# Queue orders of the middle norm in a hybrid diffusion layer: output chunks of the second half one by one, the urgent accumulator of the head units first

## The chip, the cores and the metric

One core of one Trainium2 chip. The metric is the device time of one execution in microseconds (us), the median over runs. The engines are PE (TensorE, matmuls), PEld (its weight loads), DVE (VectorE), ACT (ScalarE), POOL (GpSimd) and SP (SyncE, which issues the DMAs). Each works off its own queue in order and waits on semaphores for the others.

## The reference, cut to what matters

One layer over 128 context tokens and 512 latent tokens, width 1024. The stretch of this document lies between the two sub-layers:

```python
mod = silu(cond) @ w_ada + b_ada
sh1, sc1, g1, sh2, sc2, g2 = split(mod, 6)
...
mix = concatenate([y_ssd, u], -1) @ w_out
x = x + g1 * rms_norm(mix, norm_mix_post)
h = rms_norm(x, norm_ffn_pre) * (1 + sc2) + sh2
up = h @ w_ffn_up
up = dwconv(up)                       # 3x3 on the latent grid, 3 on the context
f = (silu(f_gate) * f_val) @ w_ffn_down
x = x + g2 * rms_norm(f, norm_ffn_post)
```

Everything is float32; the large products are made of three matmuls of split operands (high x high, high x low, low x high), so that they keep the precision.

## The kernel before, in words

Data lie transposed: 128 channels on the partitions, 640 tokens along them. A column chunk m (0 to 7) is 128 of the 1024 output channels. The tokens come in two halves, half 0 with 384 and half 1 with 256.

**The weights.** Each unit of 1024 columns is loaded by SP into `wr` (two buffers), copied by ACT into `wh` (L311), and the remainder is written to `wl` by POOL or DVE (L313). A full matmul (L415 in `mm3`, L1259 in `up_mm`) takes a 128 x 128 block of wh or wl. The units of this stretch, by the numbers that the tiles carry: wh57 and wh60 belong to chunks 3, 4 and 5, 6 of half 1 (part y), wh58, wh59, wh61, wh62 and wh64 are chunks 3 to 7 of half 1 (part u), wh63 is part y of chunk 7; wh65 to wh69 are the five head units of the up-projection; wh70 onwards are the later up units.

**The output projection and the middle norm.** For each half the chunks 3 to 7 are summed in PSUM (`y_part`, 9 matmuls, and `u_part`, 24), evicted by DVE (L1072, `out_done`), squared by ACT (L1077) and the squares added by POOL (L1079). Then, for the half:

- `msum`: column sum of the squares on PE (L473), root on ACT (L487), reciprocal on DVE (L488);
- `spread`: the row is spread over the partitions on PE (L481);
- `x2`: for each m a scaling on DVE (L1156), an add of the residual (L1158, on POOL for m = 2 and 5), a square on ACT (L1159);
- `xsum`, root, reciprocal and `spread` again;
- `h2`: for each k a scaling on DVE (L1176), the high part on ACT (L1178), the low part on DVE (L1183).

The steps for half 0 lie between the output chunks of half 1, and those for half 1 between the matmuls of the head. The head is the first five units of the up-projection; for half 0 they use the banks ps2 (unit 0), ps0, ps1, and for half 1 unit 0 uses ps2, unit 1 ps0, unit 2 ps1 and units 3 and 4 the narrow banks pq0 and pq1. Unit 0, 1 and 2 are convolved by DVE straight from PSUM (ACT L1227 starts, then ten taps, L1237 to L1240); units 3 and 4 are copied (L1262) and convolved aside by ACT and POOL (L1305, L1306). The next full unit (wh70) takes ps2 again.

**Narrow matmuls.** The adaLN products (`ada_half`, L460) and the column sums (`colsum`, L473) have only 32 output rows and are placed on one of four strips of 32 columns of the array, four strips in turn:

```python
for j in range(4):
    te.matmul(pt[32 * j:32 * j + 32, 0:P], cts[:, kc, :], w[:, j * P:(j + 1) * P],
              start=kc == 0, stop=kc == KD - 1, tile_position=(0, 32 * j))
```

**What sets the order.** Each engine's instructions are numbered in the order in which the program writes them, and `ORDER` says for each engine in which order they are issued; `issue_in_order` chains each to the one before it. In PE's order, 2927-2958 are the adaLN product 3, 2993-3024 product 4, 3059-3090 product 5 and 3539-3570 product 6; 3176-3183 and 3380-3387 are `msum` of half 0 and half 1, 3254-3269 with 3285-3300 and 3455-3470 with 3477-3492 their `xsum`; 3199-3202, 3328-3331, 3406-3409 and 3505-3508 the spreads. The chunks of half 1 are 3158-3198 (m=3), 3203-3235 (m=4), 3236-3284 (m=5), 3301-3337 (m=6) and 3338-3370 (m=7), as far as those numbers are not in the lists before. 3371-3538 are the head for half 0, 3572-3595 unit 0 for half 1, 3596-3619 unit 3, 3620-3643 unit 4, 3644-3667 unit 1, 3668-3691 unit 2; 3692-3739 is the unit of wh70.

Of the kernel before, what the change touches and what calls it, by code (L numbers as in the profile page):

```python
# [37 lines left out]
for _name, _w in (("b_ada", 48), ("g_mix_pre", 8), ("g_mix_post", 8), ("g_ffn_pre", 8),  # L38
# [37 lines left out]
2712 2683-2686 2718-2727 2687-2689 2728 2713 2729-2740 2714 2690-2692 2830-2831 2771-2780 2832-2835  # L76
2781-2790 2836-2841 2843 2741-2742 2715-2716 2792-2794 2743-2747 2791 2748-2755 2844-2847 2756-2758
2795-2799 2848-2849 2800-2809 2850-2860 2894-2896 2960-2963 2897-2915 2964-2966 2916-2924 2967-2973
2925-2926 2974-2987 2861-2892 2842 3092-3094 3026 2988-2990 3027-3035 2991-2992 3036-3045 3095 3046-3057
3096-3099 2893 3058 3125 3100-3102 2927-2942 2993-3014 2943-2950 3015-3024 2951-2958 3103-3107 2959  # L80
3108-3122 3126-3133 3123-3124 3134-3146 3203-3204 3147-3150 3025 3151-3158 3059-3089 3176-3183 3090
3159-3165 3205-3207 3166-3175 3184-3188 3208-3210 3189-3198 3211-3218 3199-3202 3091 3219-3236 3301-3310
3237-3245 3311 3246-3251 3312 3252-3253 3270-3276 3313-3317 3338 3318-3319 3277-3284 3320-3327 3332-3337
3339-3348 3254-3269 3285-3300 3328-3331 3349-3373 3388-3390 3397-3398 3380-3387 3374-3375 3399 3410-3412
3406-3409 3377 3376 3391-3393 3400-3402 3413-3415 3419 3422-3423 3378 3420 3379 3394-3396 3421 3403-3405
3424 3431 3416-3418 3425 3428 3426 3429 3432-3433 3430 3437-3439 3446-3448 3427 3434-3436 3471-3476 3443
3440-3442 3449-3451 3493-3504 3509-3510 3444-3445 3452 3511-3513 3539-3556 3455-3470 3477-3492 3514-3524
# [15 lines left out]
448-450 405-407 443 408-410 421-422 444 411 424 423 451 445-446 412-413 426 414-415 425 427 454 429-430 455  # L103
452-453 434 439 436 438 435 456 433 457 437 440 460 431 459 458 461-462 441 466-467 469-470 472 478 473
475-476 468 479-480 482-485 481 471 474 488 477 486 489 487 495 498 496 502 501 497 491 490 505 508 494
499-500 515 509 503-504 518 492 512 493 519 506-507 510-511 520-522 537 523 513-514 516 525 527-528 530 526
529 532-533 538 531 535 524 540 534 557 536 539 517 541-543 545 544 558 546 548 550 547 559 552 560-561
563-564 566 549 551 567 565 553 568 554-556 569 571-575 570 562 576-585 589 586-588 593 590 594 591-592 595
597 596 598 601-602 599-600 605 603-604 606-612 615-616 613-614 617-749 1053 750-1046 1049-1051 1047-1048
1052 1054-1063 1065 1064 1066-1075""",  # L110
    "Activation": """
0-3 7 6 4 8 5 9-11 15 18 12 19 17 21-22 13 20 24 23 25 35 26-27 32-33 14 30 28-29 16 48-49 47 31 56-58 61 64
50-51 62 34 67 65-66 63 52-53 37-38 79 116 80 54 36 39 55 71 68 40-43 120 44-45 72 46 117 121-122 81 69-70
# [14 lines left out]
498-499 494 502 496 491 497 493 505-506 509 500-501 503 507 510-511 504 512-514 516 515 508 525-526 528-529
527 521 517-518 532 519-520 531 523 522 524 530 542 541 533-536 544 543 550 537 545 538-540 547 546 559 551
548 553-554 560 556 555 549 552 557-558 561-565 568-569 566-567 570 578 571-577 581 579 583 580 603-605  # L130
609-611 582 584 588 585 615-616 632 617 586 621-622 633 590 589 634 587 643-644 638 592 623 591 645 639-640
596 593 649 624 650 598 594 597 601 599 651 595 652 606 600 602 613 607 612 608 618 614 625 619-620 627 626
630 628-629 635 631 641 636-637 646 642 653 647-648 655 654 658 656-657 660 659 663 661-662 665 664 668
666-667 670 669 673 671 675 672 674 678 676 680 677 679 683 681 685 682 684 688 686 690 687 689 693 691 695
692 694 698 696 700 697 699 703 701 727 705 702 704 708 706 709 707 714 710-713 715 719 716 725-726 717 720
731 718 723 721-722 732 724 728-729 733-734 730 735 741 736-740 745 742-744 746-747 751 748-750 752-753 757
754-756 758-759 763 760-762 764-765 769 766-768 770-771 775 772-774 776-784""",
    "Pool": """
0-13 16-19 14-15 24-25 20 26-27 33 21-23 65 69 28-30 35 70 36 34 75 51 93 31 37-42 32 49 43 50 44-48 71 97
52-59 98 64 66 72 67 77 60 76 61 73 62-63 74 80 103-104 99 78-79 81-84 92 68 105 100 85-88 94 89 123 108 90  # L140
# [4 lines left out]
219-223 239-240 224-227 241-243 232-233 244-245 234-236 246-248 251-252 249 255 250 256 253-254 257-261
264-265 267-268 262-263 266 269-270 272 271 273-274 279 275 280 276-278 281-282 294-295 300 298 285 299 303
302 304 283 315 307 286 284 316 308 287 319 309 321 320 290 324 310 323 291 325 328-329 288 293 330 289 331
296 292 301 305 297 311-312 306 314 317 313 322 326 318 332-333 327 335-336 334 338-339 337 341-342 340
344-345 343 347-348 346 350-351 349 353-354 352 356-357 355 359-360 358 362-363 361 365-366 364 367-369 372
370 373-374 371 375-377 379 378 380-381 383 382 384-385 387 386 388-389 391 390 392-393 395 394 396-397 399  # L150
398 400-411""",
    "SP": """
0-8 14 24 10 13 16 11 9 12 15 23 19 17 31 27 25 18 20 26 28-29 41 47 30 36 34-35 38 40 21 43 39 37 44-45 42
46 48-49 22 50 32-33 53 52 54-57 72 81 51 59-61 82 58 64 62 83 63 87 96 68 67 97 65-66 69 98 75-76 74 70 73
# [1442 lines left out]
```

## Time and profile before

| | |
|---|---|
| median of 3 runs | 983.82 us (982.83 to 984.3) |
| span of the profiled execution | 979.4 us |
| PE busy | 944.5 us, 96% of the span |
| DVE, ACT, POOL busy | 686.9, 471.3, 577.9 us |
| stretch that the new orders cover | about 451 to 554 us of the span |

The profiled execution's own time outside the span is not listed, so its span stands beside the median of the runs. In the profile a row of the timeline gives the start (us from the span's start), the busy time, the engine, the line, the operation, output and inputs by the program's names (without buffer numbers), the shape, and how many alike were merged; in brackets the idle time before it and what ended it. A narrow float32 matmul leaves two records.

### The profile page before, as it was taken

The numbers are of one execution on the slowest core, as the hardware profiler recorded it, in microseconds if no ns is written. First come the engines' busy times: TensorE is split into PE (matmuls) and PEld (weight loads), VectorE is DVE, ScalarE is ACT, GpSimd is POOL, SyncE is SP. The second block draws the span as 40 slices with busy tenths as digits, with TensorE's granted clock in tenths as the row PEclk, the third lists the DMA queues.
The fourth block names the chain that finished last, engine by engine and source line by source line (L and its number), as shares of the span: only waits on it lengthen the run. The fifth ranks groups of instructions, "written<-read, shape, count | busy, mean of one in ns | idle before, by whom it ended". The sixth has DMA issues, their size and how long they took to land.

```text
span 979.4 us, 18795 instructions
## 1 busy us (share of the span) xinstructions
PE 944.5 (96%) x7623; PEld 920.9 (94%) x7623; DVE 686.9 (70%) x1076; ACT 471.3 (48%) x799; POOL 577.9 (59%) x416
## 2 busy tenths in 40 slices
PE   4999999999999999999999999999999999999995
PEld 3799999999999998998889999999999999999995
DVE  1769898999989997523585998998988898400004
ACT  4355666877668477622464852323232336322211
POOL 1334699889999882534662994444454436543434
PEclk9999999999999999999999999999999999999998
DMA  9622424433424422578662322222222231322213
GB/s 347 250 72 86 117 82 127 146 95 123 139 80 142 128 91 93 196 244 303 200 218 88 129 86 69 84 78 73 86 66 86 66 87 54 94 69 76 82 38 108
DMA packets 50294, 117.52 MB, mean 120 GB/s; under 512 B 6016, under 2 KB 13952, under 8 KB 50208
## 3 DMA queue, kind: packets, MB, share of 16 engines
q1 hardware_dynamic: 50208, 116.33, 37.2%
q8 instruction: 60, 0.98, 0.4%
q14 instruction: 26, 0.21, 0.1%
HBM read 112.55 MB, written 3.75 MB: 119 GB/s over the span
## 4 chain that ended last, share of the span: by engine, by line
PE 87%; DMA 3%; ACT 3%; DVE 2%; SPq 1%; POOL 1%; issue 1%; POOLq 0%; ACTq 0%; DVEq 0%
PE ps L415 72%; PE ps L1259 3%; PE pq L415 2%; PE pq L818 2%; PE pq L807 1%; PE pq L460 1%; SPq L452 1%; DMA wr<-in_wout 1%; PE pq L744 1%; PE pq L441 1%; POOL wl L313 1%; PE pq L473 1%; DMA S<-acD 1%; ACT wh L311 1%; DMA T<-in_wada 1%
## 5 line engine op out<-in xcount | busy, mean ns | idle before, releaser
L313 POOL TENSOR_TENSOR wl<-wr,wh 128x1024 fp32r<-128x1024 f32 (+3 forms) x127 | 290.4, 2290 | 316.3 <-ACT wh L311 299.2
L415 PE MATMUL ps<-H,wh 128*128 128x384 f32 (+1 forms) x1636 | 315.7, 309 | 0.1
L311 ACT ACTIVATE wh<-wr 128x1024 fp32r<-128x1024 f32 (+3 forms) x131 | 131.3, 1003 | 316.2 <-PE ps L415 183.2
L415 PE MATMUL ps<-T,wh 128*128 128x384 f32 (+1 forms) x1472 | 272.5, 306 | 1.8 <-ACT S L1227 1.8
L1237 DVE SCALAR_TENSOR_TENSOR S<-ps,prms,S 128x441 f32<-128x441 f32 (+2 forms) x336 | 233.5, 695 | 29.4 <-ACT S L1227 18.9
L415 PEld LDWEIGHTS ps<-H,wh 128*128 128x128 f32 x1636 | 249.0, 188 | 2.7 <-issue 1.7
L415 PEld LDWEIGHTS ps<-T,wh 128*128 128x128 f32 x1472 | 218.9, 188 | 2.2 <-ACT S L1227 2.1
L872 DVE SCALAR_TENSOR_TENSOR ps<-u,prms,ps 128x655 f32<-128x655 f32 x205 | 185.1, 903 | 10.8 <-ACT ps L869 4.8
L415 PE MATMUL ps<-H,wl 128*128 128x384 f32 (+1 forms) x818 | 191.8, 309 | 0.0
L415 PE MATMUL ps<-T,wl 128*128 128x384 f32 (+1 forms) x736 | 166.2, 305 | 0.0
L415 PEld LDWEIGHTS ps<-H,wl 128*128 128x128 f32 x818 | 129.0, 188 | 1.0 <-issue 1.0
L415 PEld LDWEIGHTS ps<-T,wl 128*128 128x128 f32 x736 | 113.0, 188 | 0.0
L488 DVE RECIPROCAL rsm<-rsm 128x160 f32<-128x160 f32 (+2 forms) x9 | 7.4, 817 | 147.1 <-ACT rsm L487 147.1
L415 PE MATMUL ps<-S,wh 128*128 128x384 f32 (+1 forms) x420 | 88.0, 310 | 1.6 <-ACT wh L311 1.6
L415 PEld LDWEIGHTS ps<-S,wh 128*128 128x128 f32 x420 | 66.5, 188 | 2.8 <-ACT wh L311 1.8
L415 PE MATMUL ps<-S,wl 128*128 128x384 f32 (+1 forms) x210 | 54.9, 309 | 0.3 <-POOL wl L313 0.3
L789 ACT ACTIVATE S<-S,AC 128x128 f32<-128x128 f32 x140 | 45.5, 392 | 2.4 <-DMA S<-acD 2.4
L885 POOL TENSOR_TENSOR T<-T,T 128x640 f32<-128x640 f32 x20 | 32.0, 1602 | 12.5 <-ACT T L881 12.5
L1227 ACT ACTIVATE S<-ps,prms 128x640 f32<-128x640 f32 x42 | 36.5, 869 | 0.0
L415 PEld LDWEIGHTS ps<-S,wl 128*128 128x128 f32 x210 | 35.2, 188 | 0.9 <-POOL wl L313 0.5
L881 ACT ACTIVATE T<-u,prms 128x512 f32<-128x512 f32 (+1 forms) x54 | 27.9, 554 | 6.8 <-POOL T L885 6.8
L1339 POOL TENSOR_TENSOR H<-S,S 128x640 f32<-128x640 f32 x16 | 25.3, 1581 | 0.0
(346 smaller groups left out, 1180.3 us busy)
## 6 DMA issues: line engine op xcount, KB each, us to landing
wr<-in_wup SPq DMA_DIRECT2D x44, 512.0 KB, 3.5
wr<-in_win SPq DMA_DIRECT2D x36, 512.0 KB, 3.9
T<-in_wada SPq DMA_DIRECT2D x49, 256.0 KB, 5.4
S<-acD SPq DMA_DIRECT2D x28, 320.0 KB, 4.7
wr<-in_wdown SPq DMA_DIRECT2D x16, 512.0 KB, 3.4
wr<-in_wout SPq DMA_DIRECT2D x13, 512.0 KB, 4.5
H<-in_wada SPq DMA_DIRECT2D x23, 256.0 KB, 4.6
S<-in_wada SPq DMA_DIRECT2D x16, 256.0 KB, 5.4
```

Source lines behind the costliest of these rows:

```text
L311: ac.activation(hi[:, :n], raw[:, :n], AF.Copy)
L313: lo_eng.tensor_tensor(lo[:, :n], raw[:, :n], hi[:, :n].bitcast(F32), SUB)
L415: last_mm[0] = te.matmul(out, w, x[:, c0:c1], start=first and i == 0, stop=last and i == 2)
L789: ac.activation(rc, rc, AF.Relu, scale=-1.0, bias=AC2[:, c, row:row + 1])
L818: te.matmul(py[64 * h:64 * h + 64, i * P:(i + 1) * P], xt[:, c * P + 64 * h:c * P + 64 * h + 64], rs[h, d][:, c * P:(c + 1) * P], start=d ...
L872: ve.scalar_tensor_tensor(acc, u[:, j:j + UO], w(j), acc, MUL, ADD)
L881: ac.activation(t[:, b:c], u[:, a:a + c - b], AF.Copy, scale=w(j))
L885: gp.tensor_tensor(far, far, t, ADD)
L1227: ac.activation(out, v, AF.Identity, bias=prm_col("ffn_b", i), scale=w(1, 1))
L1237: ve.scalar_tensor_tensor(ob, vl[:, r0 + a - 1:r1 + a - 1, q0 + b - 1:q1 + b - 1], w(a, b), ob, MUL, ADD)
L1259: te.matmul(pt[:, o:o + c1 - c0], w[k] if i in (1, 2) else w[:, k * P:(k + 1) * P], x[:, c0:c1], start=k == 0 and j == 0, stop=k == KD - 1 ...
L1339: gp.tensor_tensor(f_raw[q], a, b, MUL)
```

## The change

Only the lists of `ORDER` change; every instruction, its operands and its engine stay. The five lists are laid out anew between about 451 and 554 us. In PE's list chunk 5 of half 1 is issued as a whole ahead of chunk 6; unit 0 of the head for half 1 is issued further ahead of units 1 to 4; narrow and full matmuls are mixed in another way. In ACT's list the eviction of unit 0 (579) stands ahead of the split of wh70 (581), and the squares of the norm (517-524) and the splits (529, 532) are ordered anew. In DVE's list the adds of x2 (524 to 536), the eviction of chunk 7 (558) and the parts of h2 are ordered anew. In SP's list the loads of adaLN product 5 (228-235) and 6 (262-269) and of the residual (237-244, 258-260) move against the weight loads (247-275). The diff, cut:

```diff
     "PE": """
 ...
-2925-2926 2974-2987 2861-2892 2842 3092-3094 3026 2988-2990 3027-3035 2991-2992 3036-3045 3095 3046-3057
-3096-3099 2893 3058 3125 3100-3102 2927-2942 2993-3014 2943-2950 3015-3024 2951-2958 3103-3107 2959
-3108-3122 3126-3133 3123-3124 3134-3146 3203-3204 3147-3150 3025 3151-3158 3059-3089 3176-3183 3090
-3159-3165 3205-3207 3166-3175 3184-3188 3208-3210 3189-3198 3211-3218 3199-3202 3091 3219-3236 3301-3310
-3237-3245 3311 3246-3251 3312 3252-3253 3270-3276 3313-3317 3338 3318-3319 3277-3284 3320-3327 3332-3337
-3339-3348 3254-3269 3285-3300 3328-3331 3349-3373 3388-3390 3397-3398 3380-3387 3374-3375 3399 3410-3412
 ...
-3440-3442 3449-3451 3493-3504 3509-3510 3444-3445 3452 3511-3513 3539-3556 3455-3470 3477-3492 3514-3524
-3505-3508 3557-3570 3525-3538 3453-3454 3572-3575 3644-3647 3668-3669 3576-3578 3648-3650 3670-3674
 ...
-3624-3625 3591-3593 3596-3598 3594-3595 3599-3619 3626-3643 3660-3667 3683-4059 4061-4081 4060 4082-5548
 ...
+3096-3097 3057 3098-3099 3058 3100 2927 3101 2928-2930 2893 2931-2932 3102 2933-2934 3125 2935-2941
+2993-2998 2942 2999-3008 2943 3009-3015 2944 3016-3018 2945-2950 3019-3024 2951-2952 3103 2953-2957 3104
+2958 3105-3107 2959 3108-3115 3126 3116-3122 3127 3123 3128 3124 3129-3146 3203 3147-3148 3204 3149-3150
+3025 3151-3156 3059 3157 3060-3070 3158 3071-3077 3176-3177 3078-3089 3178 3090 3179-3181 3159 3182 3160
+3205 3183 3206 3161-3165 3207 3166-3168 3208 3169-3175 3184-3188 3209-3210 3189 3211 3190-3192 3199
+3193-3198 3212 3200 3213-3218 3201-3202 3091 3219 3236 3220-3235 3237-3243 3301 3244-3253 3270-3283
+3302-3304 3284 3305-3317 3338 3318-3327 3332 3339 3333 3340-3342 3254-3255 3334-3335 3343 3336-3337
+3344-3347 3256-3266 3348 3267-3269 3285-3300 3328-3331 3349-3373 3388-3390 3397-3398 3380-3381 3374
+3382-3387 3375 3399 3410-3412 3406 3377 3407-3408 3376 3391-3392 3409 3393 3400-3402 3413-3415 3419 3378
 ...
+3437-3439 3446-3448 3427 3434-3436 3471-3473 3443 3539 3474 3540 3475-3476 3440 3541-3545 3493-3498
+3546-3551 3441-3442 3552 3449-3450 3499-3503 3455-3457 3504 3509-3510 3444-3445 3511 3553-3554 3512
+3555-3556 3452 3458-3460 3513 3451 3461-3470 3557 3477-3490 3515 3491-3492 3516 3514 3517-3523 3505-3508
+3558-3565 3524 3566-3567 3525 3568-3569 3526-3527 3570 3528-3535 3453 3536-3537 3454 3572 3538 3573
 ...
+3653-3655 3620 3656 3675-3676 3621 3677 3622-3623 3657-3658 3678 3585 3679 3586-3593 3596-3597 3594-3595
+3680 3624 3598-3605 3681 3606 3625 3607-3608 3659 3609-3613 3626 3614-3618 3660 3619 3627-3634 3682
+3635-3637 3661-3662 3638-3641 3663-3666 3683-3684 3642 3685-3688 3667 3689-3690 3692 3691 3693-3712 3643
+3713-3737 3740-3742 3738 3743-3751 3739 3752-4059 4061-4081 4060 4082-5548 5597-5615 5549-5596 5616-5658
 ...
     "DVE": """
 ...
-529 532-533 538 531 535 524 540 534 557 536 539 517 541-543 545 544 558 546 548 550 547 559 552 560-561
+529 538 532-535 540 531 536 539 516 557 517 541-543 545 558 544 546 548 550 547 559 549 552 551 560-561 563
     "Activation": """
 ...
+498-499 494 502 496 491 497 493 505 500 506 501 503 507 509 504 510-514 516 515 508 525-526 528 517 520 529
+519 523 527 518 531-532 521-522 524 530 542 533 535 541 534 544 536 543 550 545 537 539 538 540 546-547 551
+559 553 555-556 548 557 554 552 558 560-561 549 562-563 567-568 566 565 564 571-572 570 569 573 575 578 577
+574 576 579 581 580 603 605 604 584 611 609 583 616 610 615 586 617 621 585 588 582 632-633 590 589 634 587
 ...
     "SP": """
 ...
-212 246 209 223-225 218 220-222 247-248 240 239 237 231 229-230 228 234 249 233 235 242 232 250-251 243 238
+212 246 209 223-225 218 220-222 229 247 231 241 248 230 228 238 235 233-234 249 232 242 240 239 250-252 244
 ...
```

More of the change, by code (lines that the diff above doesn't have):

```diff
@@ L83 @@
-3237-3245 3311 3246-3251 3312 3252-3253 3270-3276 3313-3317 3338 3318-3319 3277-3284 3320-3327 3332-3337
-3339-3348 3254-3269 3285-3300 3328-3331 3349-3373 3388-3390 3397-3398 3380-3387 3374-3375 3399 3410-3412
-3406-3409 3377 3376 3391-3393 3400-3402 3413-3415 3419 3422-3423 3378 3420 3379 3394-3396 3421 3403-3405
-3424 3431 3416-3418 3425 3428 3426 3429 3432-3433 3430 3437-3439 3446-3448 3427 3434-3436 3471-3476 3443
-3440-3442 3449-3451 3493-3504 3509-3510 3444-3445 3452 3511-3513 3539-3556 3455-3470 3477-3492 3514-3524
@@ L88 @@
-3505-3508 3557-3570 3525-3538 3453-3454 3572-3575 3644-3647 3668-3669 3576-3578 3648-3650 3670-3674
-3579-3581 3571 3651-3653 3582-3584 3654-3656 3675-3680 3585-3587 3657-3659 3681-3682 3620-3623 3588-3590
-3624-3625 3591-3593 3596-3598 3594-3595 3599-3619 3626-3643 3660-3667 3683-4059 4061-4081 4060 4082-5548
-5597-5615 5549-5596 5616-5658 5693-5695 5659-5664 5696-5716 5665-5692 5717-6599 6665-6668 6600-6664
-6669-6676""",
+2925-2926 2974-2987 2861-2892 2842 3092-3094 3026 2988-2990 3027-3035 2991-2992 3036-3045 3095 3046-3056
@@ new lines @@
+3193-3198 3212 3200 3213-3218 3201-3202 3091 3219 3236 3220-3235 3237-3243 3301 3244-3253 3270-3283
+3302-3304 3284 3305-3317 3338 3318-3327 3332 3339 3333 3340-3342 3254-3255 3334-3335 3343 3336-3337
+3344-3347 3256-3266 3348 3267-3269 3285-3300 3328-3331 3349-3373 3388-3390 3397-3398 3380-3381 3374
+3382-3387 3375 3399 3410-3412 3406 3377 3407-3408 3376 3391-3392 3409 3393 3400-3402 3413-3415 3419 3378
+3420 3422-3423 3379 3394-3396 3421 3403-3405 3416 3424 3431 3417-3418 3425 3428 3426 3429 3432-3433 3430
@@ new lines @@
+3437-3439 3446-3448 3427 3434-3436 3471-3473 3443 3539 3474 3540 3475-3476 3440 3541-3545 3493-3498
+3546-3551 3441-3442 3552 3449-3450 3499-3503 3455-3457 3504 3509-3510 3444-3445 3511 3553-3554 3512
+3555-3556 3452 3458-3460 3513 3451 3461-3470 3557 3477-3490 3515 3491-3492 3516 3514 3517-3523 3505-3508
+3558-3565 3524 3566-3567 3525 3568-3569 3526-3527 3570 3528-3535 3453 3536-3537 3454 3572 3538 3573
+3668-3669 3574-3575 3644-3647 3576-3578 3648-3650 3670-3674 3579-3580 3651 3581 3652 3582 3571 3583-3584
@@ new lines @@
+3653-3655 3620 3656 3675-3676 3621 3677 3622-3623 3657-3658 3678 3585 3679 3586-3593 3596-3597 3594-3595
+3680 3624 3598-3605 3681 3606 3625 3607-3608 3659 3609-3613 3626 3614-3618 3660 3619 3627-3634 3682
+3635-3637 3661-3662 3638-3641 3663-3666 3683-3684 3642 3685-3688 3667 3689-3690 3692 3691 3693-3712 3643
+3713-3737 3740-3742 3738 3743-3751 3739 3752-4059 4061-4081 4060 4082-5548 5597-5615 5549-5596 5616-5658
+5693-5695 5659-5664 5696-5716 5665-5692 5717-6599 6665-6668 6600-6664 6669-6676""",
@@ L105 @@
 475-476 468 479-480 482-485 481 471 474 488 477 486 489 487 495 498 496 502 501 497 491 490 505 508 494
-499-500 515 509 503-504 518 492 512 493 519 506-507 510-511 520-522 537 523 513-514 516 525 527-528 530 526
-529 532-533 538 531 535 524 540 534 557 536 539 517 541-543 545 544 558 546 548 550 547 559 552 560-561
-563-564 566 549 551 567 565 553 568 554-556 569 571-575 570 562 576-585 589 586-588 593 590 594 591-592 595
-597 596 598 601-602 599-600 605 603-604 606-612 615-616 613-614 617-749 1053 750-1046 1049-1051 1047-1048
-1052 1054-1063 1065 1064 1066-1075""",
+499-500 515 509 492-493 503-504 512 518 506-507 519 510-511 520-522 537 523 525 513 527-528 530 524 526 514
+529 538 532-535 540 531 536 539 516 557 517 541-543 545 558 544 546 548 550 547 559 549 552 551 560-561 563
+562 564 566-567 553-556 568-569 571-572 574-577 565 579-580 573 578 581 570 582-588 590-591 598 589 592 601
+594 593 595 597 596 599-600 603-604 602 607 610 609 608 612 615 605-606 613 611 616 614 617-749 1053
+750-1046 1049-1051 1047-1048 1052 1054-1063 1065 1064 1066-1075""",
     "Activation": """
@@ L127 @@
 452-453 455 454 484-485 457 469-470 487 459 486 456 466 460 468 458 461-462 467 463-464 488-489 492 490 495
[L128 to L137, printed above, removed]
+498-499 494 502 496 491 497 493 505 500 506 501 503 507 509 504 510-514 516 515 508 525-526 528 517 520 529
+519 523 527 518 531-532 521-522 524 530 542 533 535 541 534 544 536 543 550 545 537 539 538 540 546-547 551
+559 553 555-556 548 557 554 552 558 560-561 549 562-563 567-568 566 565 564 571-572 570 569 573 575 578 577
+574 576 579 581 580 603 605 604 584 611 609 583 616 610 615 586 617 621 585 588 582 632-633 590 589 634 587
+643-644 622 638 592 623 591 645 639-640 596 593 649 624 650 598 594 597 601 599 651 595 652 606 600 602 613
+607 612 608 618 614 625 619-620 627 626 630 628-629 635 631 641 636-637 646 642 653 647-648 655 654 658
+656-657 660 659 663 661-662 665 664 668 666-667 670 669 673 671 675 672 674 678 676 680 677 679 683 681 685
+682 684 688 686 690 687 689 693 691 695 692 694 698 696 700 697 699 703 701 727 705 702 704 708 706 709 707
+714 710-713 715 719 716 725-726 717 720 731 718 723 721-722 732 724 728-729 733-734 730 735 741 736-740 745
+742-744 746-747 751 748-750 752-753 757 754-756 758-759 763 760-762 764-765 769 766-768 770-771 775 772-774
+776-784""",
     "Pool": """
@@ L144 @@
 182 228 193-195 204 196-199 206-207 231 200-201 230 229 208 213 202-203 216 212 237-238 215 217-218 214
[L145 to L151, printed above, removed]
+219-223 239-240 224-227 241-243 232-233 244-245 234-236 246-248 251-252 249 255-256 250 253-254 257 259 258
+260-261 264-265 267 262 268 263 270 266 269 272 271 273-275 279 276 280 277-278 281 294-295 300 298 303 282
+299 302 285 315 304 307 283 286 284 316 308 287 319 309 321 320 290 324 310 323 291 325 328-329 288 293 330
+289 331 296 292 301 305 297 311-312 306 314 317 313 322 326 318 332-333 327 335-336 334 338-339 337 341-342
+340 344-345 343 347-348 346 350-351 349 353-354 352 356-357 355 359-360 358 362-363 361 365-366 364 367-369
+372 370 373-374 371 375-377 379 378 380-381 383 382 384-385 387 386 388-389 391 390 392-393 395 394 396-397
+399 398 400-411""",
     "SP": """
@@ L159 @@
 198-199 191 182 197 189 183 200 217 211 204 261 210 215 207 226-227 216 206 202 208 213 205 214 236 245 219
-212 246 209 223-225 218 220-222 247-248 240 239 237 231 229-230 228 234 249 233 235 242 232 250-251 243 238
-241 252-254 244 255-256 267 263 257 270 258 260 259 271-272 264-265 269 262 266 268 273-274 276 278 280 282
-275 277 279 284 281 283 285-343 345 344 346 348 347 349 351 350 353 352 354 356 355 357 359 358""",
+212 246 209 223-225 218 220-222 229 247 231 241 248 230 228 238 235 233-234 249 232 242 240 239 250-252 244
+243 237 253-257 270 266 268 262 258 271 267 264 272 269 259 263 265 260 273-275 284-285 283 278 280-281
+286-287 277 279 282 288 276 289-343 345 344 346 348 347 349 351 350 353 352 354 356 355 357 359 358""",
 }
```

## The prediction

> **What bounds the kernel now.** I read the page first, then all of PE's waits in the stretch that the change touches, then windows and the timeline of one engine at a time.
>
> ```profile
> span 979.4 us, 18795 instructions
> ...
> PE pq L460 <- DMA T<-in_wada: 2.0, 3, 1.0
> PE ps L415 <- ACT S L1227: 1.8, 1, 1.8
> PE ps L415 <- ACT wh L311: 1.6, 1, 1.6
> PE pq L481 <- DVE gs L1127: 1.2, 1, 1.2
> PE ps L415 <- POOL wl L313: 0.3, 1, 0.3
> ...
> 500.00:541.00 41.00, 40.73 (x397) 39.24 (x396) 29.15 (x75) 21.88 (x49) 17.88 (x11) 1.00 0.47 153
> ```
>
> The span ends 979.4 us after its start; the median of the runs is 983.82, so 4.4 us lie around the span, and I add every change of the span to 983.82. The rows with arrows are those of PE between 450 and 545 us (total, times, longest): 6.9 us, all that better queue orders could win there. The last row is a window: its length, then the busy time of PE, PEld, DVE, ACT and POOL, the granted clock, the DMA share and GB/s. PE is busy for 40.73 of its 41 us, at the full clock: what is added to PE there has no cover. Behind 554 us the orders are the old ones and PE goes on without a gap, so a shift at 542 us goes through to the end.
>
> **Part 1, chunks one by one.** In half 1 the old PE order starts m=6 with ten matmuls, the tenth of which needs the weights wh62, and only then goes on with m=5, whose weights had been there.
>
> ```profile
> 483.45 0.50 PE L415 MATMUL ps<-S,wh 128*128 128x256 f32 x2 [1.59 <-ACT wh L311]
> 486.01 0.39 PE L415 MATMUL ps<-S,wl 128*128 128x256 f32 x1 [0.28 <-POOL wl L313]
> 482.34 1.06 ACT L311 ACTIVATE wh<-wr 128x1024 fp32r<-128x1024 f32 x1 [1.96 <-DMA wr<-in_wout]
> 479.45 0.40 PE L415 MATMUL ps<-H,wh 128*128 128x256 f32 x2
> 479.69 0.28 PE L415 MATMUL ps<-H,wl 128*128 128x256 f32 x1
> ```
>
> The new order puts 32 more matmuls of m=5 ahead of that tenth, at 0.12 us each (479.45 to 479.69 is two): 3.8 us of cover for a wait of 1.59, and the 0.28 behind it goes too. PE gains up to 1.9 us. SP issues the load of wr62 as soon as wl60 is made, as before; a load that I find 0.5 to 1 us earlier or later (SP now holds behind two releases of adaLN tiles) stays inside this cover.
>
> **Part 2, the urgent accumulator first.** Unit 0 sits in ps2, the bank that the next full unit needs.
>
> ```profile
> 533.78 0.27 PE L1259 MATMUL ps<-T,wl 128*128 128x256 f32 x1
> 534.03 1.06 ACT L311 ACTIVATE wh<-wr 128x1024 fp32r<-128x1024 f32 x1 [3.60 <-issue]
> 535.00 0.87 ACT L1227 ACTIVATE S<-ps,prms 128x640 f32<-128x640 f32 x1
> 535.90 5.81 DVE L1237 SCALAR_TENSOR_TENSOR S<-ps,prms,S 128x441 f32<-128x441 f32 x8 [4.23 <-ACT S L1227]
> 542.00 0.35 DVE L1240 SCALAR_TENSOR_TENSOR S<-ps,prms,S 128x127 f32<-128x127 f32 x1
> 542.49 0.82 PE L415 MATMUL ps<-T,wh 128*128 128x384 f32 x4 [1.76 <-ACT S L1227]
> ```
>
> PE finishes ps2 at 534.05, but ACT first splits wh70 (1.06) and then evicts ps2 (0.87); ten taps on DVE follow until 542.35, and PE waits 1.76 us. (The releaser named is the eviction of ps0, which happens to end at 542.4; the taps read ps2.) In the new order the eviction comes ahead of the split, 0.95 us less, and seven matmuls (0.83 us) move from ahead of the end of ps2 to behind it. From the end of ps2 the chain takes 0.1 + 0.87 + 6.45 + 0.15 = 7.55 us; PE has 61 matmuls at 0.12, 7.3 us, beside it. 0.25 us of the wait stay: **1.5 us won**. wh70 is split 1 us later and is wanted 5 us later; wh71 moves back by some 6 us behind the aside work and the eviction of unit 1; I estimate its wl at 546, wanted at 548. The matmuls of units 2 and 4 that now stand behind the waiting one delay their evictions by up to 3.5 us; DVE reaches unit 2 at 548 and unit 4 is convolved aside, much later.
>
> **Part 3, what the new PE order does to the narrow matmuls.** The adaLN products (L460) and column sums (L473) fill 32 of 128 columns of the array, four side by side. The old order has them in 6 unbroken runs of this stretch (64, 40, 32, 8, 50 and 14 instructions). The new one cuts the same 208 instructions into 32 runs with full matmuls between them, nine of them a lone instruction. Nothing in the title says so; I counted it in the two orders. Rows for full, narrow, full:
>
> ```profile
> 366.10 0.46 PE L415 MATMUL ps<-H,wh 128*128 128x256 f32 x2
> 366.49 0.48 PE L473 MATMUL ps<-T,ones 128*32 128x160 f32 x8
> 366.90 0.49 PE L807 MATMUL pq<-M,st 128*128 128x128 f32 x2
> ...
> 500.21 0.52 PE L1259 MATMUL ps<-T,wh 128*128 128x384 f32 x2
> 500.66 0.32 PE L473 MATMUL pq<-msq,ones 128*32 128x64 f32 x8
> 500.80 0.29 PE L473 MATMUL pq<-S,ones 128*32 128x64 f32 x8
> 501.02 0.62 PE L1259 MATMUL ps<-T,wh 128*128 128x384 f32 x2
> 501.49 0.34 PE L1259 MATMUL ps<-T,wl 128*128 128x384 f32 x1
> 501.66 0.51 PE L1259 MATMUL ps<-T,wh 128*128 128x384 f32 x2
> ...
> 590.84 0.45 PE L415 MATMUL ps<-T,wl 128*128 128x384 f32 x2
> 591.21 1.96 PE L460 MATMUL pq<-H,cts 128*32 128x128 f32 x64
> 593.10 0.85 PE L415 MATMUL ps<-T,wh 128*128 128x384 f32 x4
> ```
>
> Each narrow instruction leaves two records. In the last block 64 records, eight groups of four, take 1.89 us until the next full matmul: 0.22 us a group at 128 columns without the way out, so 0.27 at 160, 0.16 at 96, 0.11 at 64. A full matmul steps by 0.17 (384 columns) or 0.12 (256). What is left is the price of leaving and re-entering the full array: 366.10 to 366.90 is 0.80 - 0.24 - 0.27 = 0.29; 500.21 to 501.49 is 1.28 - 0.70 - 0.22 = 0.36; 590.84 to 593.10 is 2.26 - 0.34 - 1.76 = 0.16. The first two are runs of one and two groups, as the new ones are: I take 0.32, with 0.16 and 0.36 as ends. No row shows a run of one lone instruction; it cannot be shorter than two passes of its own, which the four take side by side, unless a lone strip runs beside full matmuls (below). A run with n instructions on its fullest strip costs n groups: the old runs have 53 groups and 9.9 us, the new ones 69 and 13.0.
>
> [...]
>
> By place:
> - Before the DMA wait at 457 us: four more runs, hidden by that wait (2.0 us in the view above). Behind it two more runs, 0.64, less an estimated 0.3, since the copy of the adaLN row (L463) no longer stands behind other ACT work: +0.3.
> - 465 to 474 (adaLN product 5 and the sum for half 0): one run becomes five, 2.07 us of groups become 2.61: 0.54 + 4 x 0.32; the spread (L481), now cut in three, 0.15 (no row shows it; half the price of a run): +2.0. So the spread ends at 480.8 instead of 478.5.
> - 500 (sum for half 1): 0.11 + 0.32 + 0.15 for its cut spread: +0.6.
> - 511 to 526 (adaLN product 6 and the second sum of half 1): two runs become fifteen, 2.83 us of groups become 4.28: 1.45 + 13 x 0.32: **+5.6**. This lies in the window where PE has no idle time.
>
> **Part 4, the middle norm of half 0 on DVE, ACT and POOL.** From the spread to the second column sum the old chain takes 478.5 to 493.7.
>
> ```profile
> 478.58 0.61 DVE L1156 SCALAR_TENSOR_TENSOR M<-M,gg,pq 128x384 f32<-128x384 f32 x1 [1.39 <-PE pq L481]
> 479.46 2.18 DVE L1156 SCALAR_TENSOR_TENSOR M<-M,gg,pq 128x384 f32<-128x384 f32 x4
> 481.56 2.15 DVE L1158 TENSOR_TENSOR M<-M,T 128x384 f32<-128x384 f32 x2
> 491.41 0.55 DVE L1158 TENSOR_TENSOR M<-M,T 128x384 f32<-128x384 f32 x1
> 480.45 2.37 POOL L313 TENSOR_TENSOR wl<-wr,wh 128x1024 fp32r<-128x1024 f32 x1 [0.97 <-ACT wh L311]
> 489.41 0.42 DVE L1072 TENSOR_TENSOR M<-ps,H 128x256 f32<-128x256 f32 x1 [1.74 <-PE ps L415]
> 491.58 1.33 ACT L1159 ACTIVATE T<-M 128x384 f32<-128x384 f32 x3
> 493.74 0.34 ACT L487 ACTIVATE rsm<-pq,epsc 128x96 f32<-128x96 f32 x1 [0.82 <-PE pq L473]
> 498.19 0.61 DVE L1183 SCALAR_TENSOR_TENSOR T<-HL,modv,T 128x384 fp32r<-128x384 f32 x1
> 498.76 0.42 DVE L1072 TENSOR_TENSOR M<-ps,S 128x256 f32<-128x256 f32 x1
> ```
>
> An add of two SBUF operands takes 0.55 us alone; while POOL makes a wl, as from 480.45, it ends only 0.4 us behind POOL (the first of the pair at 481.56 took 1.68). New walk: five L1156 from 480.8 to 483.6; the add of M0 behind POOL's wl62, to 486.2; M1 behind POOL's own add, to 487.7; M3 to 488.2; an eviction and two L1156 to 489.7; M6 behind wl63 to 490.8; the rest, with the old 1.74 us gap of DVE gone, to 492.8. On ACT the split wh64 (1.06) now stands ahead of the last three squares (0.5 each): 492.1 + 1.06 + 1.5 = 494.7, and the last sum on PE 495.1: **+1.4**. PE alone would be there at 493.7 + 2.3 - 1.9 + 0.8 = 494.9 (0.8 for two more runs), so nothing of Part 1 is left. Then the eviction of m=7 (0.42), which waits for PE's last matmul of half 1, moves from behind the first L1183 to ahead of it: 0.42 and its own wait before the first product of the head that needs that tile: **+0.8**. The root, reciprocal and spread between (the wait of 1.2) are as before.
>
> **Sum.** +1.4 + 0.8 + 0.6 + 5.6 - 1.5 = +6.9 us; 983.8 + 6.9 = **990.7**. With the low price of a run (0.16): the norm +0.6, then 0.8, 0.4, 3.5, -1.5: +3.8, 987.6. With 0.36 and the walk of Part 4 half a microsecond worse: +8.2, 992.0.
>
> **Rivals.** (a) **Faster: narrow matmuls cost nothing between full ones.** If a lone strip slips in beside the full matmuls at its share of a group (0.05 us), Parts 1 and 2 remain: 1.9 + 1.5 won, 980.4. For it: strips do run side by side, 64 records in 1.96 us. Against it: all three blocks above show the full matmul after a run late. It decides at 3.4 us over the 22 exposed extra runs, 0.15 us for each with its group. [...]
> (b) **No change: the price is right but the stretch has other slack**, or the runs cost 0.15 and the x2 chain keeps its old 15.2 us: 1.9 + 1.5 against 3.4, 983 to 985. For it: 6.9 us of waits exist. Against: none of them lies between 500 and 541.
> (c) **The orders don't bite**, because the tail of ACT and POOL holds PE at 542: POOL is busy from 535 on. Then Part 2's 1.5 us is lost, 992.2; the forecast's range holds it.
>
> **Chances.** Forecast, with (c): 0.75, 986 to 993.5. Rival (b): 0.12. Rival (a): 0.13. Within 0.2% (2 us) is about what a measurement of this kernel can't tell from no change. The range 983.5 to 993.5 leaves out (a), a part of (b) and the forecast's far end.
>
> **What would show it.** PE's busy time grows by 6 to 9 us between 450 and 541; rows of one or two narrow records between full matmuls, with 0.4 to 0.6 us from full to full; no wait on wh62 near 483; ps2 evicted ahead of wh70, and the wait on taps below 0.5 us. Wrong: full matmuls stepping by 0.12 to 0.17 across a lone narrow one, or PE's busy time unchanged.

## The result and the profile after

| | before | after |
|---|---|---|
| median of 6 runs each | 982.54 us (981.17 to 984.3) | 990.00 us (987.93 to 993.65) |
| ratio after to before, 95% interval | | 1.0081 (1.0065 to 1.0097) |
| span of the profiled execution | 979.4 us | 987.9 us |
| waits of PE between 450 and 555 us | 6.9 us | 3.5 us |

The changed kernel is 7.5 us slower by the medians and 8.5 us by the two profiled spans. In the code after, every line number is 8 higher than before. The page's span and its row of busy times:

```profile
span 987.9 us, 18790 instructions
PE 956.7 (97%) x7623; PEld 923.8 (94%) x7623; DVE 689.3 (70%) x1076; ACT 471.4 (48%) x799; POOL 576.5 (58%) x416
```

PE's busy time is the story in one number: it was 944.5 us before, and the same 7,623 matmul records now take 956.7, 12.2 us more. All of PE's waits between 450 and 555 us (total, times, longest):

```profile
PE ps L1267 <- DVE T L1191: 1.6, 2, 1.3
PE pq L489 <- DVE rsm L496: 1.2, 1, 1.2
PE ps L1267 <- ACT T L1186: 0.4, 1, 0.4
PE ps L423 <- DVE S L1248: 0.3, 1, 0.3
```

The waits on wh62 and wl62 are gone, that on the taps has shrunk from 1.76 to 0.3 us, and the DMA wait does not appear. A new one has come, 1.6 us on the h2 products (L1191). Fewer waits (3.4 us less) and a span 8.5 us longer: so the loss is inside PE's busy time. PE from the first matmuls on h2 to the first column sum of half 1 (`msum`), and then the adaLN product 6 among the head's matmuls:

```profile
499.59 0.45 PE L1267 MATMUL ps<-T,wh 128*128 128x384 f32 x1 [0.36 <-ACT T L1186]
501.38 0.44 PE L1267 MATMUL ps<-T,wh 128*128 128x384 f32 x1 [1.34 <-DVE T L1191]
...
502.39 0.54 PE L1267 MATMUL ps<-T,wh 128*128 128x384 f32 x1 [0.21 <-DVE T L1191]
502.72 0.52 PE L1267 MATMUL ps<-T,wl 128*128 128x384 f32 x1
503.04 0.84 PE L1267 MATMUL ps<-T,wh 128*128 128x384 f32 x2
503.82 0.43 PE L481 MATMUL pq<-msq,ones 128*32 128x64 f32 x4
...
516.98 0.44 PE L1267 MATMUL ps<-T,H 128*128 128x384 f32 x1
517.35 0.41 PE L468 MATMUL pq<-S,cts 128*32 128x128 f32 x2
517.68 0.63 PE L1267 MATMUL ps<-T,H 128*128 128x384 f32 x2
```

Two things are to be seen. From 516.98 to 517.68 there are one full matmul (0.17) and one narrow one by itself (a lone one, below): 0.70 us, so the lone one costs 0.53. And from 502.7 to 505.9 full matmuls step by 0.33 instead of 0.17: the granted clock there was 0.50 (502.58 to 506.00 us), as the windows in the section on the clock show.

Starts of the same PE instructions in the two profiled executions (us), and the part of the difference that arose since the row above:

| PE instruction | before | after | later by | since the row above | forecast |
|---|---|---|---|---|---|
| 3103, behind the DMA wait | 459.24 | 458.20 | -1.04 | -1.04 | 0 |
| 3202, end of the first spread | 478.15 | 479.92 | +1.77 | +2.81 | +2.3 |
| 3300, end of the second column sum | 493.41 | 493.94 | +0.53 | -1.24 | -0.9 |
| 3471, in the head behind the norm | 511.26 | 515.74 | +4.48 | +3.95 | +1.4 |
| 3570, end of the narrow runs | 523.11 | 533.55 | +10.44 | +5.96 | +5.6 |
| 3692, the matmul that waits for the taps | 542.49 | 550.84 | +8.35 | -2.09 | -1.5 |
| 6600, near the end | 959.70 | 968.22 | +8.52 | +0.17 | 0 |

### The profile page after: what moved, and what is told of

The parts are those of the page before. It is cut to its first block, busy times and chain, and to the rows that moved or that the text cites. A ratio compares the mean times of both kernels' runs of the same rounds, so it can differ in the third digit from the quotient of the medians.

```text
span 987.9 us, 18790 instructions
## 1 busy us (share of the span) xinstructions
PE 956.7 (97%) x7623; PEld 923.8 (94%) x7623; DVE 689.3 (70%) x1076; ACT 471.4 (48%) x799; POOL 576.5 (58%) x416
## 4 chain that ended last, share of the span: by engine, by line
PE 90%; DVE 3%; DMA 3%; ACT 2%; issue 1%; SPq 1%; POOL 0%; POOLq 0%; ACTq 0%; DVEq 0%
PE ps L423 74%; PE ps L1267 3%; PE pq L468 2%; PE pq L423 2%; PE pq L826 2%; PE pq L815 1%; DMA T<-in_wada 1%; PE pq L752 1%; DMA S<-acD 1%; PE pq L449 1%; DMA S<-in_wada 1%; PE pq L481 1%; DVE T L989 1%; DVE S L1245 1%; PE pq L600 1%
```

## The experiments

The theory: the loss is the narrow matmuls cut into many short runs, each of which pays for leaving and re-entering the full array; chunk order and accumulator order win what the waits were worth. Rival: the order of the other engines, the loads or the moved eviction make the loss. Every experiment changes lists of `ORDER` alone. "Before" is each time the kernel before, run on the same chip.

### The narrow runs

**The new orders, narrow runs whole.** Of the changed kernel only PE's list is touched, at six places like this one:

```diff
-3156 3059 3157 3060-3070 3158 3071-3077 3176-3177 3078-3089 3178 3090 3179-3181 3159 3182 3160 3205 3183 3206
+3156-3158 3059-3089 3176-3183 3090 3159-3160 3205-3206
```

> The new orders on all five engines, but PE's 208 narrow instructions of the stretch (adaLN products and column sums, 32 columns each) stand in six unbroken runs again (64, 40, 32, 8, 50 and 14), not in 32. Theory, the price of leaving the full array: the 6 to 8 us of narrow runs go, and the 3.4 us at half the clock from 502.6 us on, if PE's thin filling before it brought that about: 981 to 984 us. Rival, the orders of the other engines, the loads or the moved eviction of m=7 are the cause: 988 to 990, as the changed kernel.

Measured: 979.61 us against 982.45, ratio 0.9967 (0.9948 to 0.9986). So the rival falls, and the same change without the cut runs is faster than before, by more than the theory said. PE's waits between 450 and 555 us in it, but for one of 0.2:

```profile
PE pq L481 <- DVE gs L1126: 1.2, 1, 1.2
PE ps L1259 <- DVE T L1183: 1.2, 1, 1.2
PE pq L460 <- DMA T<-in_wada: 0.8, 3, 0.4
PE ps L415 <- ACT wh L311: 0.4, 1, 0.4
PE ps L415 <- DVE S L1240: 0.3, 1, 0.3
```

The wait on the taps stays at 0.3, as in the changed kernel; the granted clock is 1.00 in every window from 425 to 600 us. Against the changed kernel 10.4 us are won by this edit.

**The changed kernel, only the runs of 511 to 526 us whole.**

```diff
-3471-3473 3443 3539 3474 3540 3475-3476 3440 3541-3545 3493-3498 3546-3551 3441-3442 3552 3449-3450 ...
+3471-3473 3443 3474-3476 3440 3493-3498 3441-3442 3449-3450 3499-3504 3509-3510 3444-3445 3511-3512 3452 3513
+3451 3539-3556 3455-3470 3477-3492 3515-3516 3514 3517-3523 3505-3508 3557-3570
```

> The changed kernel with only the fifteen narrow runs between 511 and 526 us made whole again (50 and 14); the other narrow runs stay cut. Theory: the term of 5.6 us of the prediction goes (13 runs x 0.32 + 1.45 of groups): 984 to 984.5. If it is the largest part but the groups were overcounted: 986. Rival, the cut runs before 500 us carry the loss: 988 to 990.

Measured: 985.16 us against 981.95, ratio 1.0031 (1.0012 to 1.005): between the first two answers, 4.8 us under the changed kernel. In the trace 3471 to 3570 takes 11.67 us, against 17.81 in the changed kernel and 11.85 before; at 3692 it is 6.15 us ahead of the changed kernel, of which 0.54 was there at 3471: 5.6 for this place. Its one profiled execution was granted 0.66 of the clock from 500 to 510 us, the changed kernel's 0.83: two stretches of 3.4 us at half the clock where the other has one, an estimate from these two numbers. What remains above the regrouped kernel (985.2 to 979.6) lies before 511 us.

**Before, with those two runs alone cut.**

```diff
-3471-3476 3443 3440-3442 3449-3451 3493-3504 3509-3510 3444-3445 3452 3511-3513 3539-3556 3455-3470 ...
+3471-3476 3443 3539-3540 3440 3541-3545 3441-3442 3449-3451 3493-3498 3546-3552 3499-3503 3455-3457 3504
+3509-3510 3444-3445 3452 3511 3553-3554 3512 3555-3556 3458-3470 3557 3477-3490 3513-3515 ...
```

> The kernel before, with PE's two narrow runs between 511 and 526 us alone cut into ten (21 groups of four in the place of 17), between the same full matmuls as in the new order; all other engines as before. Theory: 8 runs x 0.32 us + 4 groups x 0.2 us = +3.4 us (2.1 to 3.8 by the two ends of the price). Rival, narrow instructions slip in between full ones for nothing: 0, and full matmuls that step by 0.17 us across a lone narrow one.

Measured: 985.38 us against 982.45, ratio 1.0021 (0.9998 to 1.0045). The interval just holds no change, so the total does not settle it. The trace does: 3471 to 3570 takes 16.14 us instead of 11.85, 4.3 more, of which 0.5 is a load that came late for the earlier first instruction:

```profile
513.54 0.41 PE L456 MATMUL pq<-S,cts 128*32 128x128 f32 x4 [0.50 <-DMA S<-in_wada]
513.88 0.44 PE L1255 MATMUL ps<-T,wh 128*128 128x384 f32 x1
```

The remaining 3.8 is the upper end of the expectation.

**One run of 32 cut into lone instructions, and into groups of four.** Both edit the run at 591 us, where PE is never idle; ACT's copy of the product (612) and one transpose (4060) move behind it.

```diff
-4026-4059 4061-4081 4060 4082-4097
+4026-4028 4061 4029 4062 4030 4063 4031 4064 4032 4065 4033 4066 4034 4067 4035 4068 ...      lone
+4026-4031 4061 4032-4035 4062 4036-4039 4063 4040-4043 4064 4044-4047 4065 4048-4051 ...      fours
```

> The kernel before, with adaLN product 7 (one run of 32 narrow instructions at 591 us, in a stretch where PE is never idle) cut into 31 runs, 30 of them one lone instruction between full matmuls. Theory: 30 more runs x 0.32 us + 23 more groups x 0.22 us = +14.7 us (9.9 to 15.9 by the two ends). If a lone strip costs a run but no whole group: +9.6. Rival, lone strips run beside full matmuls: within 1 us of before.

> As the cut of adaLN product 7 into lone instructions, but into eight runs of one whole group of four each: the groups stay 8, only the number of runs grows from 1 to 8. Theory: 7 x 0.32 = +2.2 us (1.1 to 2.5). Rival, only the groups left unfilled cost: 0.

Measured: lone 997.12 us against 982.45, +14.7, ratio 1.0149 (1.0106 to 1.0191); fours 984.99, +2.5, ratio 1.0027 (1.0009 to 1.0045). Lone, then fours (start, length, records; two records are one instruction):

```profile
594.50 0.45 PE L413 MATMUL ps<-T,wh 128*128 128x384 f32 x1
594.87 0.41 PE L458 MATMUL pq<-H,cts 128*32 128x128 f32 x2
595.21 0.39 PE L413 MATMUL ps<-T,wh 128*128 128x256 f32 x1
595.53 0.41 PE L458 MATMUL pq<-H,cts 128*32 128x128 f32 x2
595.86 0.44 PE L413 MATMUL ps<-T,wh 128*128 128x384 f32 x1
```

```profile
593.99 0.44 PE L411 MATMUL ps<-T,wh 128*128 128x384 f32 x1
594.35 0.43 PE L456 MATMUL pq<-H,cts 128*32 128x128 f32 x8
594.71 0.39 PE L411 MATMUL ps<-T,wh 128*128 128x256 f32 x1
595.02 0.42 PE L456 MATMUL pq<-H,cts 128*32 128x128 f32 x8
595.38 0.44 PE L411 MATMUL ps<-T,wl 128*128 128x384 f32 x1
```

From full to full over two narrow runs and two full matmuls (0.17 + 0.12), lone takes 1.36 us and fours 1.39: (1.36 - 0.29) / 2 = 0.535 and 0.55 for each run. One strip alone costs as much as four side by side. With 0.22 for a group, the price of a run is 0.32 to 0.33. The two totals come from this place: from 3787, ahead of it, to 6600 the traces take 14.6 and 2.4 us more than before. What takes the time inside that price, no run here shows.

### Chunks and accumulators by themselves

**Before, with m=5 whole ahead of m=6.**

```diff
-3219-3236 3301-3310 3237-3245 3311 3246-3251 3312 3252-3253 3270-3276 3313-3317 3338 3318-3319 3277-3284 ...
+3219-3253 3270-3284 3301-3327 3332-3348
```

> The kernel before, with only PE's order of half 1 changed: all of m=5, then all of m=6, then m=7 (the narrow runs stay whole, all other engines as before). The waits of 1.59 and 0.28 us on wh62 and wl62 go. Theory A, PE itself holds the second column sum of the middle norm: -1.9 us at that sum and at the end, some 980.5. Theory B, the prediction's walk of DVE, ACT and POOL holds it: the last narrow instruction of that sum stays at 493.4, the time at 982 to 982.5.

Measured: 982.03 us against 981.95, ratio 1.0004 (0.9987 to 1.002). The number is theory B's, and its reason is there at the end: the column sum waits 0.49 us for ACT's squares (the last row). But a new wait of PE stands ahead of it:

```profile
479.34 5.03 POOL L307 TENSOR_TENSOR wl<-wr,wh 128x1024 fp32r<-128x1024 f32 x2 [1.53 <-ACT wh L305]
481.76 0.39 PE L409 MATMUL ps<-S,wl 128*128 128x256 f32 x1 [1.47 <-POOL wl L307]
479.88 4.91 DVE L1152 TENSOR_TENSOR M<-M,T 128x384 f32<-128x384 f32 x2
491.86 0.79 PE L467 MATMUL pq<-T,ones 128*32 128x96 f32 x24 [0.49 <-ACT T L1153]
```

PE's wait on wh is down to 0.3 us in the view of waits, and in its place stands one of 1.5 us on a wl that POOL makes: 5.03 us for two in a row. Beside them two adds of the norm on DVE take 4.91 us, 2.15 in the kernel before, and the squares come behind these adds. So the gain goes to POOL's wl and to the walk that theory B names; from 3103 to 3300 the stretch takes 34.84 us, 34.17 before (34.45 and 35.22 in the kernels with the runs of 511 to 526 cut and with ps2 evicted first, which keep the old order there). With all the new orders (the regrouped kernel) that wait is absent and one of 0.4 us on wh remains: there the stretch from 3103 to 3300 is 0.87 us shorter than before (33.30 against 34.17).

**Before, with ps2 evicted first.** ACT's list has 579 ahead of 581, and in PE's list seven matmuls move:

```diff
-... 3675-3680 3585-3587 3657-3659 3681-3682 3620-3623 3588-3590 3624-3625 3591-3593 3596-3598 3594-3595 3599-3609
+... 3675-3679 3585-3587 3657-3658 3620-3623 3588-3593 3596-3597 3594-3595 3598 3624-3625 3659 3680-3682 3599-3602
```

> The kernel before, with only the end of unit 0 changed: ACT evicts ps2 ahead of the split wh70, and seven matmuls of other units stand behind the end of ps2. The wait of 1.76 us at 540.7 should shrink to 0.25: -1.5 us, some 981. If only the swap on ACT counts: -0.95. If the wait is not the taps' but that of the eviction of ps0, which the trace names: 0.

Measured: 981.85 us against 981.95, ratio 0.9996 (0.9981 to 1.0011). The wait is gone, and most of it is given back 8 us later:

```profile
541.17 0.82 PE L410 MATMUL ps<-T,wh 128*128 128x384 f32 x4
541.91 0.87 ACT L1222 ACTIVATE S<-ps,prms 128x640 f32<-128x640 f32 x1
548.72 1.21 ACT L1300 ACTIVATE U<-H,prms 128x448 f32<-128x448 f32 x2
549.42 0.82 PE L410 MATMUL ps<-T,wh 128*128 128x384 f32 x4 [0.83 <-ACT U L1300]
```

From 3570 to 3692 PE wins 1.71 us; from 3692 to 3787 it loses 1.35, of which the wait shown is 0.83. This also answers whose wait it was: the eviction that stood as releaser (L1222 here) ends at 542.78, and PE goes on at 541.17 without it; it was the taps. In the regrouped kernel the loss between 3692 and 3787 is 0.42, in the changed kernel 0.12.

**Both together.**

> The kernel before with the two edits of the title and nothing else of the change: PE's chunk order of half 1, and ps2 evicted ahead of wh70 with seven matmuls behind it. By the prediction's Parts 1 and 2 -3.4 us. By the two runs of each part alone (0.1 and -0.1): 0, since the wait on wh62 turns into one on wl62 from POOL, and what is won at 542 is given back by 556.

Measured: 981.08 us against 982.16, ratio 0.9989 (0.997 to 1.0008): no difference that this measurement can tell. Its trace shows both new waits at once:

```profile
PE ps L409 <- POOL wl L307: 1.4, 1, 1.4
PE ps L409 <- ACT U L1299: 0.8, 1, 0.8
```

So the two edits that the title names show no gain by themselves. In the regrouped kernel, with the new orders of ACT, POOL, DVE and SP around them, neither of the two waits stands in PE's view above; that these orders are what the edits lack is argued from that, and no run adds them one by one.

### The eviction of m=7

**The regrouped kernel, with the eviction put back behind the first product.** One swap in DVE's list:

```diff
-545 558 544 546
+545 544 558 546
```

> The new orders with the narrow instructions in six whole runs (measured 979.6, -2.8), and besides the eviction of m=7 (DVE) behind the first product of the middle norm's second tile of the head (L1183 in the kernel before) instead of ahead of it, as in the kernel before. Theory: the wait of 1.2 us of PE on that product goes: 978.4, -4.0 against before. Rival, the eviction is then late for the norm of half 1: no gain, 979.6.

Measured: 979.21 us against 981.95, ratio 0.997 (0.9954 to 0.9987): as the regrouped kernel, which is the rival's number. Its reason is not seen: the column sum of half 1 starts without a wait (3380, at 504.02 us). In the trace the wait of 1.2 at that place is down to 0.3 (3370 to 3372 takes 0.46 us, 1.64 without the swap), but 3372 to 3380 takes 2.70 instead of 1.61. PE now waits for a later h2 product of DVE (at 502.51 us) and for a split of ACT (at 503.64): the steps there are 0.56 and 0.35 us longer than back to back.

### The clock

The stretches at half the clock were not in any forecast, and they lie at other places from one profiled execution to the next (from 502.58 us in the changed kernel, 484.88 in the run in fours); in that of the kernel before the granted clock is 1.00 from 30 to 971 us. Windows of 3.41 us of PE (length, busy, granted clock, DMA share, GB/s), for after, for before, for before with the runs of 511 to 526 cut, and for the run in fours:

```profile
499.17:502.58 3.41, 1.50 (x6) 1.00 0.95 330
502.58:506.00 3.42, 3.42 (x23) 0.50 0.38 124
```

```profile
480.38:483.80 3.42, 1.83 (x16) 1.00 0.30 121
483.80:487.21 3.41, 3.13 (x27) 1.00 0.49 139
```

```profile
544.73:548.14 3.41, 1.65 (x11) 1.00 0.84 246
548.14:551.56 3.42, 3.42 (x15) 0.50 0.66 232
```

```profile
481.46:484.88 3.42, 1.08 (x9) 1.00 0.19 54
484.88:488.29 3.41, 3.41 (x19) 0.50 0.51 152
```

The three stretches in which PE was busy for 1.08, 1.50 and 1.65 of 3.41 us are each followed by one of equal length at 0.50 of the clock; the one with 1.83, before, is not. To test that as a cause, ACT got two splits ahead of the square root for which PE waits:

```diff
-524 530 542 533 535 541 534 544 536 543 550
+524 542-543 530 533 535 541 534 544 536 550
```

> The new orders with six whole narrow runs (979.6), and two splits of ACT (wh65 and wh66, 1.05 us each) ahead of the square root of the middle norm at 491.8, so that PE's wait there grows from 1.2 to 3.3 us. It tests what the half-clock stretches follow: in ten profiled executions a stretch of 3.413 us at half the clock came after nearly every stretch of that length in which PE was busy for under 0.52 of it, and after none over 0.56. If that is the cause: half the clock for 3.4 us right behind the gap, mean clock lower by 0.002, and +2.1 for the wait + 1.7 for the clock, 983.4. If the half-clock stretches fall at random: +2.1, 981.7, and no such stretch at 495.

Measured: 990.41 us against 982.16, ratio 1.0086 (1.0052 to 1.012), +10.8 against the regrouped kernel: the size was missed. The second split waited 3.2 us for its load, and PE's gap became 6.1 instead of 3.3 us:

```profile
PE pq L481 <- DVE gs L1126: 6.1, 1, 6.1
PE ps L1259 <- DVE T L1183: 2.1, 1, 2.1
```

```profile
492.15:495.56 3.41, 0.00 (x0) 1.00 0.46 154
495.56:498.97 3.41, 1.68 (x8) 0.50 0.71 223
498.97:502.39 3.42, 3.42 (x18) 0.50 0.33 84
502.39:505.80 3.41, 1.34 (x10) 1.00 0.23 54
505.80:509.21 3.41, 3.41 (x25) 0.50 0.89 314
```

The place and the sequence are as the cause demands: each stretch with 0.00, 1.68 and 1.34 us of work has one at 0.50 behind it, the full one at 498.97 has one at 1.00. The mean clock of its four runs is 0.988 to 0.990, against 0.994 to 0.997 in the ten of the regrouped kernel. Of the time, 5.5 us arose from 3300 to 3331 (7.73 against 2.25), and 3.6 from there to 3471 (20.66 against 17.05), where the half clock lies beside longer waits on h2. What the half clock costs by itself is not measured here: no run has the same gap without a half-clock stretch behind it.

## Why the prediction was right

The forecast was 990.7, the median is 990.0, and the mechanism that was to decide it, the cut runs, is shown: whole runs turn the same orders from 990.0 into 979.6. Some terms met, some missed in both directions.

**Part 3, met.** The price of 0.32 us a run and a whole group for a lone strip gave +14.7 and +2.2 for the two cuts at 591 us; measured +14.7 and +2.5. The 5.6 us for 511 to 526 are 5.6 between the traces with this place cut and whole, and +5.96 from before to after. The 2.3 up to the first spread measured 2.81, of which 2.48 go when the runs are whole (21.72 and 19.24 us from 3103 to 3202). The cut spread, put at 0.15 from no row, costs under 0.1: in the regrouped kernel it takes 2.27 us with 13 matmuls at 0.12 between its parts, 0.64 whole. The sign given beforehand, 6 to 9 us more of busy PE between 450 and 541, came out larger: 12.2 over the span, with the time of the vanished waits and the half clock in it.

**Part 4, first term: met, by the other arm of the working.** The second column sum was to end 1.4 us later. Counted from the instruction behind the DMA wait, it ends 1.57 later (0.53 + 1.04). The view of waits has none of PE between the first spread and that sum in after: what held the sum there is PE with its cut runs (the 494.9 that the prediction gives as PE's own), not the walk of DVE, ACT and POOL (495.1). In the trace, too, the two lie close: ACT's last square ends at 493.10 and PE starts the last run of that sum at 493.17, with no wait listed before it:

```profile
491.77 1.33 ACT L1167 ACTIVATE T<-M 128x384 f32<-128x384 f32 x3
493.17 1.02 PE L481 MATMUL pq<-T,ones 128*32 128x96 f32 x38
```

The working had them 0.2 us apart, so the number came out by either: that it met is luck as far as the reason goes, which was the wrong one of the two. The walk was put 1.6 us too late: 494.7 for the last square, with a spread that ended 0.9 later than it did. With the runs whole both start earlier, the spread by 2.5 us and the sum by 2.5 (477.39 and 491.45).

**Part 4, second term, with the sum for half 1: missed.** +0.8 and +0.6 were forecast from 493.9 to 515.7, and +3.95 came. The wait on the h2 products is the one with the eviction ahead of them, but undoing that order won nothing: the h2 chain holds PE either way, 1.0 us more than before in the regrouped kernel (3300 to 3387 takes 8.45 us, 7.45 before). Another 0.6 were forecast for the cut sum. Most of the rest is put down to the clock: 3.42 us at 0.50 in a stretch where PE is busy throughout are up to 1.7 us. No step of the prediction had the clock; it took the 1.00 of before as given.

**Part 1, too large.** 1.9 us were promised to PE where nothing else held; alone the edit won 0, since POOL's wl took the place of wh and the squares came no earlier, and with all orders 0.87. "A cover of 3.8 us" was counted for the split on ACT; the POOL instruction behind it was taken to go along. In the sum nothing of this part was left, so the total was not hurt.

**Part 2, met where it was put.** -1.5 forecast; -1.56 in the regrouped kernel and -2.09 in the changed one between 3570 and 3692, with 0.3 us of the wait left (0.25 forecast; the parts of that chain add up to 7.57, not 7.55, which changes nothing). That "a shift at 542 us goes through to the end" holds only with the new orders behind: alone, 1.35 of 1.71 us were given back by 556.

**The baseline.** The sum was set on 983.82, the median of three runs; six runs gave 982.54 and up to 35 gave 981.95 to 982.45. By ratio the change is 0.0081 x 982.5 = 8.0 us (6.4 to 9.5), against 6.9 forecast, which lies inside that interval. What is missing has about the size of the clock's part, and a baseline 1.3 us high hid it: that the absolute time met to 0.7 us is luck in part. The mean granted clock fits: 0.993 is the median of the runs after, 0.994 to 0.995 before; 0.0015 of 980 us is 1.5 us, an estimate.

**Rivals.** (a) falls: no row has a full matmul stepping undisturbed past a narrow one, and 30 lone strips cost 14.7 us. (b) falls: 3.4 us of waits went, and making the runs whole wins 10.4 back. (c) did not occur; the wait on the taps is 0.3 us. Once the runs are whole the other orders are worth 2.8 us, near the 3.4 that Parts 1 and 2 gave together: the best kernels here are the regrouped one (0.9967) and the one with the eviction put back besides (0.997). Where the 2.8 come from is open in part: from 3103 to the end of the span the profiled executions differ by 0.66 us (519.50 against 520.16), since the h2 chain and the stretch behind 3692 take back most of what Parts 1 and 2 win.

## What to carry to other kernels

When an order is changed, count not only which instruction waits for what but how often the engine goes from full matmuls to narrow ones and back: here 26 more runs of narrow matmuls between full ones, at 0.32 to 0.33 us a run in the cuts at 591 us, cost more than the 3.4 us of waits that the new order removed. Removing a wait won nothing here where the next producer in the chain (POOL behind ACT, the aside work behind the eviction) was late by as much (982.03 and 981.85 us against 981.95), so look for what ends second. And look at the clock behind a gap on PE: in the changed kernel 3.42 us at 0.50 follow one, up to 1.7 us more by the estimate above.

## What the runs showed of the hardware

**Half the clock came behind stretches with little PE work.** In the profiled execution of the changed kernel the granted clock goes to 0.50 or back to 1.00 at 24.72, 28.13, 502.58, 506.00 and 980.45 us: 3.41, 474.45, 3.41 and 474.45 us apart, which is 1, 139, 1 and 139 times 3.413. With the time of each of the twelve profiled executions laid out in stretches of that length from its first clock record, and the first 13 us and the end left out (some 3,300 stretches): all 14 in which PE's matmuls covered at most 0.523 were followed by half the clock; of 7 between 0.526 and 0.56, two were; of those above, only one, which was itself at half the clock. Eleven of these stretches:

| execution | window from (us) | PE busy of 3.41 us | granted clock in the next 3.41 us |
|---|---|---|---|
| two splits ahead of the root | 492.15 | 0.00 | 0.50 |
| regrouped, eviction put back | 171.35 | 0.86 | 0.50 |
| run in fours | 481.46 | 1.08 | 0.50 |
| two splits ahead of the root | 502.39 | 1.34 | 0.50 |
| changed | 499.17 | 1.50 | 0.50 |
| before, runs of 511 to 526 cut | 544.73 | 1.65 | 0.50 |
| two splits ahead of the root (itself at 0.50) | 495.56 | 1.68 | 0.50 |
| changed | 21.31 | 1.78 | 0.50 |
| before | 480.38 | 1.83 | 1.00 |
| before, ps2 evicted first | 481.27 | 1.91 | 1.00 |
| changed | 492.35 | 2.17 | 1.00 |

The wait of PE of 1.8 us for the taps stands both in the kernel before and in the one with the runs of 511 to 526 cut. In the first the granted clock stays 1.00 from 526 to 570 us; in the second 3.42 us at 0.50 follow (from 548.14 us), up to 1.7 us of PE's work by the estimate above.

**A narrow instruction by itself between full matmuls costs 0.535 us**, as much as a group of four (0.55) and three times a full matmul of 384 columns (0.17), though it takes a quarter of the columns (128*32 against 128*128).
